# Output projection of a two-layer hybrid trunk: one chunk each of four groups first, with their last states gated before the final scans

## The chip, the core and the metric

One core of a Trainium2 chip runs the whole program: TensorE (PE, with its weight loads listed as PEld), VectorE (DVE), ScalarE (ACT), GpSimd (POOL) and SyncE (SP), which issues the DMAs of the stretch treated here. The metric is the device time of one execution in microseconds (us). The kernel before takes 2250.49 us (median of three runs, 2247.55 to 2251.17).

## The reference

Layer 0 is a gated linear attention, layer 1 an RG-LRU. Only the end of layer 1 matters here:

```
proj = h @ w_in                        # h: [2048 latent + 256 context, 1024]
z, g = split(proj, [1280])
z = conv4(z) + bias
r, i = sigmoid(z @ w_a + b_a), sigmoid(z @ w_x + b_x)     # 5 blocks of 256 channels
a = exp(-8 * r * softplus(-lam));  u = sqrt(1 - a*a) * (i * z)
h_t = a_t * h_{t-1} + u_t              # forwards (hf) and backwards (hb), column-major over the grid
y = ((hf + hb) * silu(g)) @ w_out      # [2048, 1280] @ [1280, 1024]
out = x + gate * rms_norm(y)
```

The latent grid has 32 rows and 64 columns; the scans run column by column, so position `32*c + r` of a scanned channel is row r of column c.

## The kernel before

All products are made in three matmuls of split operands (`mm_step`, L272 to L275: hi x hi, hi x lo, lo x hi). Channels lie on partitions: the 1280 channels are five blocks `b` of two tiles each, so w_out has ten slices k = 0 to 9 (`NLT`), two per block, and each slice has two halves `nh` of 512 output columns. The 2048 rows of the output are eight groups `g` of 256 (four grid rows each); a group has two chunks `i` of 128 rows: i = 0 takes grid columns 0 to 31, i = 1 columns 32 to 63.

**Block by block.** For each block, `proj_block` projects z and the gate branch g (one unit `u` of rows after another; the copies of the g part go through tiles tagged `gs`, L1057, and are stored to `g1d`, L1058), `mix` makes the two scans, and `gate` (blocks 0 to 3 only) multiplies silu(g) with the summed states and stores to `ogd`. `mix` of block b runs woven into `proj_block` of block b+1. `mix` has two directions d of two halves hb each: it makes the r and i gates piece by piece (PE, then sigmoids at L979), then for the whole half tanh, sqrt and exp on ACT (each kind behind a table load), two products on DVE (L1158, L1159), and the scans (L1166 forwards, L1170 backwards). The backward scan adds its result to `hf` (L1175). In the backward direction the half hb = 0 covers grid columns 32 to 63 and hb = 1 columns 0 to 31.

**Partial sums.** While `mix` of the last block (b = 4) runs, `part_gen` sums k = 0 to 3 (`KPART` = 4) for all 16 chunks and stores the partial results to `ypd`. Its activations come in pages: `og_page` (L1199 on) loads a page of two k-slices of 256 rows from `ogd` into a tile `gs` (named og, L1210), casts it on ACT (hi, L1212), subtracts on DVE (lo, L1214). The hi and lo tiles lie in the pool `wA` (32 buffers), next to the slices of w_out. The pool `p3` gives `gs` two buffers, and the pages, the copies of `proj_block` and whatever else carries the tag share these two. For the last block (b = 4) nothing is stored: `og_page` loads `g1d` (L1204), applies Silu (L1205), multiplies with the rows of `hf` (L1208) and then splits.

**The weave.** `weave(prev, part_gen(), 1.0)` takes one step of `mix`, then one of `part_gen`. `mix` has 18 steps; step 17 of `part_gen` is the first of group 4, in which it asks for the two pages of group 5 and for slices 7 and 8 of w_out. The last stretch of `mix` (the tables and scans of d = 1, hb = 1) is `mix`'s step 18. The rest of `part_gen`, with the pages of groups 6 and 7, is written out after it.

**Order.** The program's text gives the order of tile requests; the framework then fixes, before the run, the order of the instructions of each engine from a simulated timeline, so an engine may run instructions well ahead of or behind the text. A tile gets one of its tag's buffers when one is free.

**The end.** Eight PSUM banks (`banks`) are filled with k = 4 to 7 of chunks 0 to 3 (groups 0 and 1) before the last block's pages exist (`pre`). Then the loop over groups adds k = 8, 9 for these, makes k = 4 to 9 for the others, and finishes each chunk: add the partial sum (L1310), multiply by the gate row (L1311), sum of squares on ACT (L1314), the rstd (L165 to L177), add x (L1323), store.

Of the kernel before, what the change touches and what calls it, by code (L numbers as in the profile page):

```python
# [9 lines left out]
F32 = mybir.dt.float32  # L10
F32R = mybir.dt.float32r
I32 = mybir.dt.int32
AF = mybir.ActivationFunctionType
ALU = mybir.AluOpType
# [3 lines left out]
P = 128  # L18
# [45 lines left out]
def kernel(ctx, tc, x, c, cx, c_ctx, ada_w, ada_b, norm_pre, norm_post,  # L64
# [17 lines left out]
    def mk(p, tag, shape, dtype=F32, bufs=None, name=None):  # L82
        uid[0] += 1
        kw = {} if bufs is None else {"bufs": bufs}
        return p.tile(list(shape), dtype, tag=tag, name=f"{name or tag}_{uid[0]}", **kw)
# [186 lines left out]
    def mm_step(o_, a, b, first, last):  # L272
        PE.matmul(o_, a[0], b[0], start=first, stop=False)  # L273
        PE.matmul(o_, a[0], b[1], start=False, stop=False)  # L274
        PE.matmul(o_, a[1], b[0], start=False, stop=last)  # L275
# [682 lines left out]
    if True:  # L958
# [27 lines left out]
        def load_wo(p, k, tag="w"):  # L986
            return [load_split(p, lru_w_out[0, k * P:(k + 1) * P, nh * 512:(nh + 1) * 512], [512], tag, name="wo")
                    for nh in range(2)]
# [107 lines left out]
        def mix(b, zs, pend, res):  # L1096
# [3 lines left out]
            for d in range(2):  # L1100
# [5 lines left out]
                for hb, pieces in enumerate(halves):  # L1106
# [39 lines left out]
                    if d == 0 and hb == 0:  # L1146
                        yield from pend
                        hf = [mk(qh, "hf", [P, T]) for t in range(2)]
                    TT = [mk(q1, "TT", [P, 1280], bufs=2) for t in range(2)]
                    kts = [2 * b + t for t in range(2)]  # L1150
                    for t in range(2):
# [5 lines left out]
                    for t in range(2):  # L1157
                        V.scalar_tensor_tensor(TT[t][:, 0:n], R[t][:, 0:n], 1.0, TT[t][:, 0:n], op0=ALU.add, op1=ALU.mult)  # L1158
                        V.tensor_tensor(I[t][:, 0:n], I[t][:, 0:n], TT[t][:, 0:n], op=ALU.mult)  # L1159
                    for t in range(2):  # L1160
                        for (a, w), o_ in zip(pieces, offp):
                            init = 0.0 if tail[t] is None else tail[t]
                            ac, ic = R[t][:, o_:o_ + w], I[t][:, o_:o_ + w]
                            if d == 0:
                                dst = hf[t][:, a - TC:a - TC + w] if a >= TC else ic
                                V.tensor_tensor_scan(out=dst, data0=ac, data1=ic, initial=init, op0=ALU.mult, op1=ALU.add)  # L1166
                                last = dst[:, w - 1:w]
                            else:
                                rv = [[-1, w]]
                                V.tensor_tensor_scan(out=vw(ic, w - 1, rv), data0=vw(ac, w - 1, rv), data1=vw(ic, w - 1, rv),  # L1170
                                                     initial=init, op0=ALU.mult, op1=ALU.add)
                                last = ic[:, 0:1]
                                if a >= TC:
                                    fs = hf[t][:, a - TC:a - TC + w]
                                    V.tensor_tensor(fs, fs, ic, op=ALU.add)  # L1175
                            tc_ = mk(q1, "tail", [P, 1], bufs=4)
                            V.tensor_copy(tc_, last)
                            tail[t] = tc_
# [21 lines left out]
        def og_page(p, g, b, pp, tag, nb=None):  # L1200
# [13 lines left out]
            V.tensor_tensor(lo, og, hi[:].bitcast(F32), op=ALU.subtract)  # L1214
            return hi, lo

        og0, wo = [], []
        for d in range(2):
            load_gate_w(0, d)
# [12 lines left out]
    with ExitStack() as s4:  # L1232
        pa = pool(s4, "p4a", 4, side="right")
        wpr = pool(s4, "wp4r", 4, side="right")

        def part_gen():

            sp = og0[0:2]
            for g in range(T // GT):
                nxt = None  # L1240
                if g + 1 < T // GT:
                    nxt = [og_page(p, g + 1, b_, wA, "w") for b_ in range(KPART // 2)]
                else:
                    og0.extend(og_page(p, 0, b_, wA, "w") for b_ in range(KPART // 2, NB - 1))
                if g == 0:
                    for k in range(KPART, 7):
                        wo.append(load_wo(wA if k < 6 else wpr, k))
                if g == T // GT // 2:

                    for k in (7, 8):  # L1250
                        wo.append(load_wo(qg, k, tag="gw"))
                for i in range(2):
                    n = 2 * g + i
                    for nh in range(2):
                        tg, nb = ("sc", 1) if (2 * n + nh) % 4 == 3 else ("pj", 3)
                        py = mk(ps, tg, [P, 512], bufs=nb)
                        mm3(py, [tuple(pg[:, k % 2, i * P:(i + 1) * P] for pg in sp[k // 2]) for k in range(KPART)],
                            [wo[k][nh] for k in range(KPART)])
                        yt = mk(pa, "yp", [P, 512])
                        (S.copy if nh else V.tensor_copy)(yt, py)  # L1260
                        st(ypd[n][:, nh * 512:nh * 512 + 512], yt)
                        yield
                sp = nxt

        weave(prev, part_gen(), 1.0)
        s5.close()
        del stages[3:]


        banks = [("pj", 3)] * 3 + [("uo", 2)] * 2 + [("sc", 1), ("sb", 1), ("tr", 1)]  # L1270

        def share(py, sp, i, nh, ks):
            for k in ks:
                mm_step(py, tuple(pg[:, k % 2, i * P:(i + 1) * P] for pg in sp[(k - KPART) // 2]), wo[k][nh],
                        k == KPART, k == NLT - 1)

        def bank(j):
            tg, nb = banks[j % 8]
            return mk(ps, tg, [P, 512], bufs=nb)

        sps = [og0[2:], [og_page(p, 1, b_, wA, "w") for b_ in range(KPART // 2, NB - 1)]]
        wo.append(load_wo(wA, 9))
        pre = []
        for n in range(4):
            for nh in range(2):
                pre.append(bank(len(pre)))
                share(pre[-1], sps[n // 2], n % 2, nh, range(KPART, 8))
        p = pool(s4, "p4", 2)
        grow = mk(p, "grow0", [P, 2, 512], bufs=1)
        ld(grow.rearrange("p a b -> p (a b)"), g1r)  # L1290
        pages = lambda g: (sps[g] if g < 2 else []) + [og_page(p, g, b_, p, "oh", 14)
                                                       for b_ in range(NB - 1 if g < 2 else KPART // 2, NB)]
        nxt = pages(0)
        for g in range(T // GT):
            sp, nxt = nxt, pages(g + 1) if g + 1 < T // GT else None
            for i in range(2):
                n = 2 * g + i
                xt = mk(p, "xt", [P, D])
                rows_of = lambda ap: ap.rearrange("(r c) d -> c r d", r=4)[32 * i:32 * i + 32]
                ld(xt, rows_of(x1d[g]))  # L1300
                yt = mk(p, "yt", [P, 2, 512])
                yf = yt.rearrange("p a b -> p (a b)")
                s2_ = mk(p, "s2", [P, 1], bufs=4)
                yp = mk(p, "ypl", [P, 2, 512])
                ld(yp.rearrange("p a b -> p (a b)"), ypd[n])
                for nh in range(2):
                    j = 2 * n + nh
                    py = pre[j] if j < 8 else bank(j)
                    share(py, sp, i, nh, range(8 if j < 8 else KPART, NLT))
                    V.tensor_tensor(yp[:, nh], py, yp[:, nh], op=ALU.add)  # L1310
                    V.tensor_tensor(yt[:, nh], yp[:, nh], grow[:, nh], op=ALU.mult)  # L1311
                jk = mk(p, "jk", [P, D], mybir.dt.bfloat16)
                if n + 1 < T // P:
                    S.activation(jk, yp.rearrange("p a b -> p (a b)"), AF.Square, accum_out=s2_)  # L1314
                else:
                    sh = mk(p, "sh", [P, 2], bufs=1)
                    for nh in range(2):
                        S.activation(jk[:, nh * 512:nh * 512 + 512], yp[:, nh], AF.Square, accum_out=sh[:, nh:nh + 1])
                    V.tensor_tensor(s2_, sh[:, 0:1], sh[:, 1:2], op=ALU.add)
                rs = rstd_of(p, s2_, 1, 1.0 / D, "yn")  # L1320
                w = D if n + 1 < T // P else 512
                for o_ in range(0, D, w):
                    V.scalar_tensor_tensor(yf[:, o_:o_ + w], yf[:, o_:o_ + w], rs, xt[:, o_:o_ + w], op0=ALU.mult, op1=ALU.add)  # L1323
                    st(rows_of(out[0][g * GT:(g + 1) * GT])[:, :, o_:o_ + w], yf[:, o_:o_ + w])
# [31 lines left out]
```

## Time and profile before

| | us |
|---|---|
| median of three runs | 2250.49 |
| profiled execution, device time | 2249.55 |
| its span, first to last instruction | 2247.8 |
| PE busy in the span | 2159.2 (96%) |
| DVE busy | 1683.7 (75%) |
| ACT busy | 1333.8 (59%) |
| mean granted TensorE clock | 0.987 |

The share of busy time is an average over stages. The change touches only the last 300 us, so the profile is read there: first the busy time by stretches, then the order in time of the engines around each hole in PE's work. In a timeline a row gives the start, the duration, the engine, the line, the operation, the tiles (out<-in), and in brackets the idle time before it with what ended it. "issue" rows of SP are the time in which the DMA was put into its queue, not its transfer.

### The profile page before, as it was taken

To read this page: it belongs to the slowest core of one execution; us is meant where nothing else is said; L and a number is where in the kernel's file an instruction comes from. 1 tells how busy PE (TensorE), PEld (TensorE's weight loads), DVE (VectorE), ACT (ScalarE), POOL (GpSimd) and SP (SyncE) were. 2 spreads that over 40 slices of the span, in tenths; PEclk is the share of its full clock that TensorE was granted. 3 is DMA by queue.
4 is the path that set the end of the run, shared out by engine and by line. 5 is a ranking of instruction groups with operands and counts; after the bars stand their busy time and mean duration, and the time that the engine had idled before them with its cause. 6 is when DMAs were issued, how large, how long until landed. Compare 5 with 4: busy or idle time off the path is not lost.

```text
span 2247.8 us, 40378 instructions
## 1 busy us (share of the span) xinstructions
PE 2159.2 (96%) x14935; PEld 1769.1 (79%) x14935; DVE 1683.7 (75%) x4043; ACT 1333.8 (59%) x2508; POOL 83.5 (4%) x173
## 2 busy tenths in 40 slices
PE   6999999999999999989999999999999999999898
PEld 3888888888877887877777788878887878777686
DVE  3898988898876987958887235684686766967687
ACT  4767676665544554545776436756757757747531
POOL 1000000000000000000000000000000000000000
PEclk9999999999999999999999999999999999999999
DMA  9322233344245324367886862365354463442276
GB/s 311 125 94 99 91 110 126 114 129 130 87 169 171 126 99 154 125 226 244 280 284 217 297 238 98 136 216 197 104 190 148 131 213 125 159 164 99 90 259 227
DMA packets 212725, 370.93 MB, mean 165 GB/s; under 512 B 22818, under 2 KB 90624, under 8 KB 212528
## 3 DMA queue, kind: packets, MB, share of 16 engines
q1 hardware_dynamic: 202544, 336.61, 44.9%
q0 software_dynamic: 9120, 30.44, 3.6%
q8 instruction: 117, 1.92, 0.3%
q10 hardware_dynamic: 864, 1.31, 0.2%
q14 instruction: 80, 0.66, 0.1%
HBM read 250.54 MB, written 117.74 MB: 164 GB/s over the span
## 4 chain that ended last, share of the span: by engine, by line
PE 73%; DVE 9%; DMA 8%; ACT 7%; issue 2%; SPq 0%; DVEq 0%; ACTq 0%
PE pj L273 15%; PE pj L274 15%; PE pj L275 15%; PE uo L273 3%; PE uo L275 3%; PE uo L274 3%; DMA h<-h0d 2%; PE sc L538 2%; ACT TT L979 2%; DMA TT<-g1d 2%; ACT L979 1%; PE sc L273 1%; PE sc L274 1%; PE sc L275 1%; PE tr L261 1%
## 5 line engine op out<-in xcount | busy, mean ns | idle before, releaser
L274 PE MATMUL pj<-h,w 128*128 128x256 f32 (+1 forms) x1120 | 372.8, 333 | 7.8 <-DMA h<-h0d 5.5
L273 PE MATMUL pj<-h,w 128*128 128x256 f32 (+1 forms) x1120 | 373.1, 335 | 3.8 <-ACT zc L1054 2.2
L275 PE MATMUL pj<-h,w 128*128 128x256 f32 (+1 forms) x1120 | 370.1, 331 | 0.0
L274 PEld LDWEIGHTS pj<-h,w 128*128 128x128 f32 x1120 | 212.5, 190 | 33.1 <-DMA h<-h0d 7.7
L273 PEld LDWEIGHTS pj<-h,w 128*128 128x128 f32 x1120 | 212.6, 190 | 30.0 <-ACT zc L1054 2.5
L273 PE MATMUL pj<-w,h 128*128 128x512 f32 (+1 forms) x592 | 232.0, 394 | 0.0
L274 PE MATMUL pj<-w,h 128*128 128x512 f32 (+1 forms) x592 | 230.7, 390 | 0.0
L275 PE MATMUL pj<-w,h 128*128 128x512 f32 (+1 forms) x592 | 229.8, 388 | 0.0
L275 PEld LDWEIGHTS pj<-h,w 128*128 128x128 f32 x1120 | 212.3, 190 | 19.9
L273 PE MATMUL pj<-wo,oh 128*128 128x512 f32 x424 | 173.0, 409 | 16.8 <-ACT oh L1212 9.2
L551 ACT ACTIVATE E<-E 128x512 f32<-128x512 f32 x216 | 135.1, 632 | 75.0 <-DVE E L548 71.0
L274 PE MATMUL pj<-wo,oh 128*128 128x512 f32 x424 | 169.6, 400 | 0.0
L275 PE MATMUL pj<-wo,oh 128*128 128x512 f32 x424 | 168.6, 401 | 0.1
L552 DVE TENSOR_TENSOR E<-QK,E 128x512 f32<-128x512 f32 x216 | 142.4, 682 | 4.4 <-ACT E L551 4.0
L275 PEld LDWEIGHTS pj<-w,h 128*128 128x128 f32 x592 | 111.2, 188 | 21.6
L273 PEld LDWEIGHTS pj<-w,h 128*128 128x128 f32 x592 | 111.0, 188 | 21.6
L274 PEld LDWEIGHTS pj<-w,h 128*128 128x128 f32 x592 | 111.3, 188 | 20.8
L546 DVE TENSOR_TENSOR E<-xc 128x256 f32<-128x256 f32 (+1 forms) x252 | 100.6, 399 | 29.6 <-PE tr L584 17.1
L1158 DVE SCALAR_TENSOR_TENSOR TT<-R,TT 128x1280 f32<-128x1280 f32 (+1 forms) x40 | 52.5, 1355 | 91.7 <-ACT R L979 91.7
L273 PEld LDWEIGHTS pj<-wo,oh 128*128 128x128 f32 x424 | 80.7, 190 | 37.3 <-ACT oh L1212 9.7
L1142 DVE TENSOR_TENSOR I<-I,zc 128x512 f32<-128x512 f32 (+1 forms) x100 | 62.9, 632 | 57.8 <-ACT I L979 57.3
L979 ACT ACTIVATE TT<-TT 128x512 f32<-128x512 f32 (+2 forms) x72 | 65.3, 926 | 59.9 <-DMA TT<-g1d 59.2
(353 smaller groups left out, 5269.7 us busy)
## 6 DMA issues: line engine op xcount, KB each, us to landing
h<-h1d SPq DMA_DIRECT2D x296, 256.0 KB
defd<-de POOLq DMA_DIRECT2D x64, 320.0 KB, 2.6
de<-defd SPq DMA_DIRECT2D x64, 320.0 KB
h0d<-h SPq DMA_DIRECT2D x72, 256.0 KB
h<-h0d SPq DMA_DIRECT2D x72, 256.0 KB
h1d<-h SPq DMA_DIRECT2D x72, 256.0 KB
xt<-in_x_dram SPq DMA_DIRECT2D x32, 512.0 KB
xt<-in_ada_w_dram SPq DMA_DIRECT2D x32, 512.0 KB
```

Source lines behind the costliest of these rows:

```text
L261: PE.transpose(to, xh[i][kk * P // w][:, kk * P % w:kk * P % w + P], ident if mixed is None else mixed)
L273: PE.matmul(o_, a[0], b[0], start=first, stop=False)
L274: PE.matmul(o_, a[0], b[1], start=False, stop=False)
L275: PE.matmul(o_, a[1], b[0], start=False, stop=last)
L538: PE.matmul(dst, lk[:, i * P + w * a:i * P + w * a + w], lq[:, i * P + w * b:i * P + w * b + w], start=True, stop=True, tile_position=(0, ...
L546: V.tensor_tensor(vw(E, s, [[256, nq], [2 * s, nb], [1, s]]), vw(X, 1 + s, [[256, nq], [2 * s, nb], [1, s]]), vw(X, s, [[257, nq], [2 * s, ...
L551: S.activation(E, E, AF.Exp, scale=-1.0 / 16)
L552: V.tensor_tensor(E, QK, E, op=ALU.mult)
L979: ins = S.activation(*a, **kw).ins
L1142: V.tensor_tensor(I[t][:, o_:o_ + w], I[t][:, o_:o_ + w], zsl(t, a, w), op=ALU.mult)
L1158: V.scalar_tensor_tensor(TT[t][:, 0:n], R[t][:, 0:n], 1.0, TT[t][:, 0:n], op0=ALU.add, op1=ALU.mult)
```

## The change

- `og_half` is a page of the last block for one chunk: 128 rows of both k-slices instead of 256. It loads through a `gs` tile of whichever pool `p` names at that time, applies Silu, multiplies with the rows of `hf` of this chunk alone, and puts hi and lo into one tile.
- `early` makes the four halves i = 1 of groups 0 to 3. It is called in `mix` of the last block, in its last half (d = 1, hb = 1), ahead of the scans. Their hi and lo tiles take the four `gw` buffers that the backward gate weights leave. At that place `p` is the pool `p3`.
- Slice 8 of w_out moves from `gw` to `wA`, and is loaded with slice 9 after the pages.
- Ahead of the last loop, the pages k = 4 to 7 of groups 0 to 3 are made (before: groups 0 and 1), and the eight banks take chunk i = 1 of groups 0 to 3 instead of both chunks of groups 0 and 1: first k = 4 to 7 for all, then k = 8, 9 from the early halves.
- The last loop finishes these four chunks first, then chunk 0 of groups 0 to 3, then groups 4 to 7. The halves i = 0 are made in the first four turns.

```diff
@@ mix
                         hf = [mk(qh, "hf", [P, T]) for t in range(2)]
+                        hf_now[:] = [hf]
...
                         V.tensor_tensor(I[t][:, 0:n], I[t][:, 0:n], TT[t][:, 0:n], op=ALU.mult)
+                    if b == NB - 1 and d + hb == 2:
+                        early()
                     for t in range(2):
@@ new
+        def og_half(pp, tag, nb, g, i):
+            og = mk(p, "gs", [P, 2, GT], name="og")[:, :, 0:P]
+            ld(og, g1d[NB - 1][:, :, g * GT + i * P:g * GT + i * P + P])
+            S.activation(og, og, AF.Silu)
+            for t in range(2):
+                orow = og[:, t].rearrange("p (c r) -> p c r", r=4)
+                V.tensor_tensor(orow, orow, vw(res[0][t], 4 * g + 32 * i * ROWS, [[ROWS, 32], [1, 4]]), op=ALU.mult)
+            pg = mk(pp, tag, [P, 2, 2, P], F32R, bufs=nb, name="oh")
+            S.copy(pg[:, 0], og)
+            V.tensor_tensor(pg[:, 1], og, pg[:, 0].bitcast(F32), op=ALU.subtract)
+            return pg
+        def early():
+            res.append(hf_now[0])
+            for g in range(4):
+                halves[g, 1] = og_half(qg, "gw", 8, g, 1)
+            res.clear()
@@ part_gen
-                    for k in (7, 8):
-                        wo.append(load_wo(qg, k, tag="gw"))
+                    wo.append(load_wo(qg, 7, tag="gw"))
@@ after the weave
-        sps = [og0[2:], [og_page(p, 1, b_, wA, "w") for b_ in range(KPART // 2, NB - 1)]]
-        wo.append(load_wo(wA, 9))
-        for n in range(4):
+        full[0] = og0[2:]
+        for g in range(1, 4):
+            full[g] = [og_page(p, g, b_, wA, "w") for b_ in range(KPART // 2, NB - 1)]
+        for k in (8, 9):
+            wo.append(load_wo(wA, k))
+        for g in range(4):
             for nh in range(2):
                 pre.append(bank(len(pre)))
-                share(pre[-1], sps[n // 2], n % 2, nh, range(KPART, 8))
+                share(pre[-1], g, 1, nh, range(KPART, 8))
+        for g in range(4):
+            for nh in range(2):
+                share(pre[2 * g + nh], g, 1, nh, range(8, NLT))
...
+        order = [(g, 1) for g in range(4)] + [(g, 0) for g in range(4)] + [(g, i) for g in range(4, 8) for i in range(2)]
+        for n_, (g, i) in enumerate(order):
+            if 1 <= n_ < 5:
+                halves[n_ - 1, 0] = og_half(p, "oh", 14, n_ - 1, 0)
+            if n_ in (5, 7, 9, 11):
+                full[(n_ + 3) // 2] = [og_page(p, (n_ + 3) // 2, b_, p, "oh", 14) for b_ in range(KPART // 2, NB)]
```

## Rows read from the trace of the kernel before

**Rows 1.** Busy time by stretch, all engines; the first line names the columns.

```profile
core 0: us, PE busy (x) PEld busy (x) DVE busy (x) ACT busy (x) POOL busy (x), PEclk, DMA share, GB/s
2110.00:2120.00 10.00, 6.11 (x27) 4.59 (x25) 8.49 (x10) 4.94 (x6) 0.00 (x0) 0.94 0.10 35
2120.00:2130.00 10.00, 4.66 (x13) 3.70 (x14) 6.51 (x13) 1.24 (x2) 0.00 (x0) 0.55 0.46 162
```

**Rows 2.** Timeline of PE: around its last hole, and its last matmul.

```profile
2115.71 0.40 PE L275 MATMUL tr<-wo,oh 128*128 128x512 f32 x1
...
2125.34 0.79 PE L273 MATMUL pj<-wo,oh 128*128 128x512 f32 x1 [9.23 <-ACT oh L1212]
...
2129.24 0.39 PE L274 MATMUL uo<-wo,oh 128*128 128x512 f32 x1
...
2238.70 0.39 PE L275 MATMUL tr<-wo,oh 128*128 128x512 f32 x1
```

**Rows 3.** Chain of waits ahead of that matmul: start, us, what.

```profile
2100.85 0.69 DVE hf L1175
...
2113.87 2.27 DVE I L1159 x2
...
2123.92 0.68 DVE og L1208 x2
2124.67 0.63 ACT oh L1212
```

**Rows 4.** Timeline of ACT: uses of the two gs buffers, 1857 to 1946 us.

```profile
1857.83 0.60 ACT L1057 COPY gs<-sc 128x512 f32<-128x512 f32 x1
...
1913.71 1.08 ACT L1057 COPY gs<-pj 128x512 f32<-128x512 f32 x2
...
1922.73 0.61 ACT L1212 CAST oh<-og 128x512 fp32r<-128x512 f32 x1
...
1945.81 1.05 ACT L1057 COPY gs<-pj 128x512 f32<-128x512 f32 x2
```

**Rows 5.** Instructions on tile og: xcount, duration ns min/median/max; DMA to landing (tile gs).

```profile
L1212 ACT CAST oh<-og x40: 603/620/633, 1921.6 to 2206.4; 128x512 fp32r<-128x512 f32 x40
L1214 DVE TENSOR_TENSOR oh<-og,oh x40: 665/683/694, 1923.1 to 2210.4; 128x512 fp32r<-128x512 f32 x40
L1208 DVE TENSOR_TENSOR og<-og,hf x16: 414/418/426, 2123.8 to 2205.9; 128x256 f32<-128x256 f32 x16
DMA to landing us min/median/max: 2.0/2.8/6.7
```

**Rows 6.** Timeline of SP: stores from gs, loads of pages, loads of w_out.

```profile
1869.81 2.87 SPq L198 DMA_DIRECT2D stg<-in_lru_w_out_dram  x2
...
1914.33 0.81 SPq L1058 DMA_DIRECT2D g1d<-gs  x2
...
1918.04 1.29 SPq L1210 DMA_DIRECT2D og<-ogd  x2
...
1928.70 16.02 SPq L198 DMA_DIRECT2D stg<-in_lru_w_out_dram  x6
...
1949.31 1.28 SPq L1210 DMA_DIRECT2D og<-ogd  x2
...
2020.46 0.54 SPq L1210 DMA_DIRECT2D og<-ogd  x1
...
2028.73 0.53 SPq L1210 DMA_DIRECT2D og<-ogd  x1
```

**Rows 7.** Timeline of PE: last matmul of group 5's partial sums, first of group 6's.

```profile
2049.25 0.40 PE L275 MATMUL sc<-wo,oh 128*128 128x512 f32 x1
2049.49 0.39 PE L273 MATMUL pj<-wo,oh 128*128 128x512 f32 x1
```

**Rows 8.** Timeline of ACT: behind the last exp of the last half.

```profile
2112.53 1.28 ACT L1205 ACT_TABLE_LOAD   x1
2113.83 1.15 ACT L1205 ACTIVATE og<-og 128x512 f32<-128x512 f32 x2
```

More of the change, by code (lines that the diff above doesn't have):

```diff
@@ L1215, in og_page @@
             return hi, lo
+        def og_half(pp, tag, nb, g, i):
[9 more added lines that the diff above has]
+            return pg
+        halves = {}
+        def early():
[3 more added lines that the diff above has]
+            res.clear()
+        hf_now = []
         og0, wo = [], []
@@ L1270, with share @@
         banks = [("pj", 3)] * 3 + [("uo", 2)] * 2 + [("sc", 1), ("sb", 1), ("tr", 1)]
-        def share(py, sp, i, nh, ks):
+        full = {}
+        def share(py, g, i, nh, ks):
             for k in ks:
-                mm_step(py, tuple(pg[:, k % 2, i * P:(i + 1) * P] for pg in sp[(k - KPART) // 2]), wo[k][nh],
-                        k == KPART, k == NLT - 1)
+                if k >= KPART + 4 and (g, i) in halves:
+                    pg = halves[g, i]
+                    act_ = (pg[:, 0, k % 2], pg[:, 1, k % 2])
+                else:
+                    act_ = tuple(q[:, k % 2, i * P:(i + 1) * P] for q in full[g][(k - KPART) // 2])
+                mm_step(py, act_, wo[k][nh], k == KPART, k == NLT - 1)
         def bank(j):
@@ L1290 @@
         ld(grow.rearrange("p a b -> p (a b)"), g1r)
[L1291 to L1296, printed above, removed]
+        order = [(g, 1) for g in range(4)] + [(g, 0) for g in range(4)] + [(g, i) for g in range(4, 8) for i in range(2)]
[4 more added lines that the diff above has]
+                full[(n_ + 3) // 2] = [og_page(p, (n_ + 3) // 2, b_, p, "oh", 14) for b_ in range(KPART // 2, NB)]
+            if True:
                 n = 2 * g + i
@@ L1306 @@
                 for nh in range(2):
-                    j = 2 * n + nh
-                    py = pre[j] if j < 8 else bank(j)
-                    share(py, sp, i, nh, range(8 if j < 8 else KPART, NLT))
+                    j = 2 * n_ + nh
+                    if j < 8:
+                        py = pre[j]
+                    else:
+                        py = bank(j)
+                        share(py, g, i, nh, range(KPART, NLT))
                     V.tensor_tensor(yp[:, nh], py, yp[:, nh], op=ALU.add)
```

## The prediction

> **What bounds the kernel now.** I read the busy time by stretches first, then PE's timeline, then the chain of waits, then the timelines of SP and ACT. PE is full nearly everywhere in the last 200 us, except in one hole: 6.11 of 10 us busy in the one stretch and 4.66 in the next, where the granted clock falls to 0.55 [rows 1]. PE stops at 2116.1 us, when the eight banks hold all that needs no last state, and goes on at 2125.34, after 9.23 us of waiting for a cast of ScalarE [rows 2]. Ten matmuls then take 3.90 us up to 2129.24, the first of them at half clock; from there to 2239.1 there are 470 matmuls, 0.2337 us each, so the slow ones cost 3.90 - 2.34 = 1.6 us. The hole is worth 9.2 + 1.6 = 10.8 us at most. The chain in front of it is the second half of the last backward scan: product L1159, scans, multiplication with `hf` (L1208), cast (L1212) [rows 3]. But the states of columns 32 to 63 are final far earlier, with the last L1175 of the first half, at 2101.5 us. The change works on these.
>
> **Part 1, the aim.** No matmul is added or removed: 96 go into the banks for k = 4 to 7 as before, and 48 (4 groups x 2 halves x 2 slices x 3) become ready ahead of the last scans, 11.2 us at 0.2337. They would cover the hole of 9.2. This is the gain that can be had; whether it comes is decided by part 2.
>
> **Part 2, the two `gs` buffers.** Each early half first needs a `gs` tile of pool `p3`, which has two, and its text stands ahead of the pages of groups 6 and 7. What does the trace say of the order in which buffers are given? The copies of the g part left both buffers by about 1861 (1857.83 and 0.60, and a store of 2.8 us [rows 4, 5]), and the next copies came at 1913.71. In between both buffers were empty for 50 us, and the first two pages, whose data in `ogd` were long complete, were not loaded: their loads come at 1918.04, just behind the stores of the copies that precede them in the text. SP was not the reason; it issued loads of w_out, which stand later in the text, at 1869.81 [rows 6]. The same a second time: casts of these pages at 1922.73, next copies at 1945.81, next pages only at 1949.31, six loads of w_out in between [rows 4, 6]. So the buffers of one tag are given in the order of the text, even while they lie empty.
>
> In the text the early halves (step 18 of `mix`) stand behind step 17 of `part_gen`, which asks for group 5's pages, and ahead of all of its later steps. Before, two loads take the buffers at 2020.46 and 2028.73: group 6's pages, the thirteenth and fourteenth loads of the twenty before the hole [rows 6]. After, these places belong to early halves 0 and 1, whose inputs in `g1d` are complete. They then sit in both buffers until `hf` is final, near 2100, and halves 2 and 3 come next in the same buffers. Only behind them come group 6's pages. PE finishes group 5's partial sums at about 2049.5 and begins group 6's there [rows 7]; it would have only gate matmuls from then on.
>
> **When does PE go on?** The first half's states are final at 2101.5 [rows 3]. Without the pages of groups 7, 0 and 1, DVE loses six L1214 of 0.68 = 4.1 us before that; against this, Silu of two halves brought forward between sigmoids costs a table load there and one back, each 1.30 from its start to the next instruction [rows 8], at two moments, 5.2 us. That bounds it between 2097.4 and 2106.7; I take 2099, nearer the lower end since a Silu can also stand in a wait. Then:
> - Halves 0, 1: each two multiplications of half the size of L1208 (0.42; between 0.21 and 0.42, I take 0.3), a cast of half of 0.62 (0.4) and a subtraction of half of 0.68 (0.42) [rows 5]: 1.4 us for the first, 2100.4.
> - Halves 2, 3: transfer 2.8 [rows 5], 2103.2. Silu early at a table load of 1.30 and 0.4, then 1.4: 2106.3. Or Silu behind the exps as in the trace [rows 8]: DVE is then at L1159, which ends at 2116.1 - 2.5 = 2113.6, and 1.4 more gives 2115.1 [rows 3].
> - Group 6's first page: transfer 2.8, cast 0.62, subtraction 0.68 = 4.1: 2110.4 or 2119.2.
>
> The two ends lie equally near to rows; I take 2115.
>
> **The sum.** From group 6 on PE has 96 matmuls of partial sums, 96 for the banks and 480 for the rest, 672 x 0.2337 = 157.0 us, and 1.6 of slow clock after the halt. End of PE: 2115 + 158.6 = 2273.6. Before, its end is 2239.1 in a span of 2247.8; the same 8.7 us behind it give a span of 2282.3, and the 1.75 us between span and the profiled execution's time (2249.55) give 2284.1. The median of the runs, 2250.49, is 0.9 above that execution; I leave this in the range. **Forecast: 2284 us.**
>
> In this sum the hole of 9.2 us is already gone: by the time that the banks are full the last scans are long over. What is late next are the pages: a pair takes 4.1 to 5 us through two buffers, and PE needs a new pair each 24 matmuls, 5.6 us, so it should not stop again. The extra pages of groups 2 and 3 (4 casts, 4 subtractions) then lie beside PE's partial sums, at nothing if DVE keeps up, else 4 x 0.68 = 2.7 us. Slice 8 in `wA` instead of `gw` is loaded beside the same sums: nothing, or a wait of one transfer, 2.8. The halves instead of pages in the last loop are four more issues on SP (0.53 each [rows 6]) of half the bytes, behind PE's 432 remaining matmuls: nothing, or 2.1. The transfers of the last loop (rows of x, partial sums, results) are the same.
>
> A rule weighed: a table load for Silu shows 1.30 us to the next instruction [rows 8]. The Trainium skill, "ScalarE: Activation LUTs", section "What ACT_TABLE_LOAD costs", counts 2.66 us for each switch, a drain included. By that the late way would take 1.36 more, and the sum about 2285; this trace doesn't show the drain.
>
> **Rivals.**
> 1. *Buffers go to whom is ready* (other side: faster). Then group 6 keeps its pages and the early halves get buffers later. Silu stands behind the exps, L1159 ends at 2116.1, the first half is ready 1.4 later at 2117.6, and PE waits 1.5 instead of 9.2 and keeps its clock: 2249.55 - 7.7 - 1.6 = 2240. The later halves come in time (2.8 us of matmuls for each group). The four halves put 4 x 1.02 = 4.1 us ahead of the scans, which end at 2128, when the 48 matmuls end also, at 2128.8. For it: the aim of part 1 is sound. Against: both empty stretches of part 2. It decides at whether a page load (L1210 before) for group 6 is issued by about 2035. 2238 to 2246.
> 2. *No difference*: as in 1, but Silu is drawn into the sigmoids at two moments, 5.2 us, and the 4.1 ahead of the scans falls on the end of the chain: 9.3 against 9.3, 2250.
> 3. *Slower still*: after the halt, DVE takes the scans and L1159 ahead of the pages' subtractions. The scans of the last half fill 2116.1 to 2123.9; a page behind them lets PE start at 2125 or later, and one more wait of the pages of up to 8 us follows: 2294 to 2304.
>
> **Chances.** The forecast with its own range, 2275 to 2295 (start of PE at 2106 to 2126): 0.65. Rival 1: 0.15. Rival 2: 0.05. Rival 3: 0.15. A measurement of this kernel can tell about 0.2%, 4.5 us, from no change. So faster 0.15, same 0.05, slower 0.80. The range 2266 to 2304 holds the forecast's case and rival 3, with some room below for a start of PE as early as 2098; the faster cases are left out.
>
> **What would show it.** Right: in the timeline of SP two loads og<-g1d of the early halves near 2020 and 2029, none of og<-ogd between there and 2100; PE with gate matmuls only from about 2050 to 2115, at a low clock; then no hole until the end. Step by step: last L1175 of the first half near 2099; group 6's first partial sum near 2115; last matmul near 2274. Wrong: group 6's sums at 2050 as before, and early casts near 2117. Then rival 1 holds, and what failed is the reading that buffers follow the text.

## The result and the profile after

| | before | after |
|---|---|---|
| median of 4 runs, us | 2250.83 | 2288.92 |
| lowest to highest, us | 2247.55 to 2256.91 | 2285.48 to 2296.77 |
| profiled execution, device time | 2249.55 | 2292.11 |
| its span | 2247.8 | 2290.3 |
| PE busy | 2159.2 (96%) | 2172.6 (95%) |
| mean granted TensorE clock | 0.987 | 0.976 |

The changed kernel is slower: 1.0174 times the time of before, with a 95% interval of 1.0155 to 1.0194. The forecast was 2284.

Two profiled executions can't be laid over each other by their start, since executions of one kernel differ by more than 10 us and some of that arises in program text that is the same. I use a mark instead: the last stores of the g part (the issue g1d<-gs behind the copies of 1945.81 [rows 4]). It is at 1946.41 us before and at 1955.03 after. "Aligned" below means: after's time less 8.62. From the mark to the end of the span are 301.4 us before and 335.3 after, 33.9 more; the medians differ by 38.1. A figure "from the mark on" always comes from the one execution that was profiled, and its own spread is not known.

SP after, the loads of tile og alone. L1213 is the load of a page, L1223 that of a half; compare [rows 6], where two pages were loaded at 2020.46 and 2028.73:

```profile
2005.62 0.53 SPq L1213 DMA_DIRECT2D og<-ogd  x1
2013.01 0.53 SPq L1213 DMA_DIRECT2D og<-ogd  x1
...
2027.54 0.54 SPq L1223 DMA_DIRECT2D og<-g1d  x1
...
2037.52 0.53 SPq L1223 DMA_DIRECT2D og<-g1d  x1
...
2103.85 1.30 SPq L1223 DMA_DIRECT2D og<-g1d  x2
...
2120.35 10.10 SPq L1213 DMA_DIRECT2D og<-ogd  x5
```

No page is loaded between 2013 and 2120. PE's timeline after, some matmuls with waits ahead of them, and its last; L1215 is the cast of a page:

```profile
2088.68 0.79 PE L273 MATMUL uo<-zh,gw 128*128 128x512 f32 x1 [6.74 <-ACT R L979]
...
2102.82 0.79 PE L273 MATMUL sb<-zh,gw 128*128 128x512 f32 x1 [3.35 <-ACT I L979]
2124.19 0.80 PE L273 MATMUL pj<-wo,oh 128*128 128x512 f32 x1 [18.44 <-ACT oh L1215]
...
2281.49 0.40 PE L275 MATMUL tr<-wo,oh 128*128 128x512 f32 x1
```

The wait of 9.23 us for a page of the last block, at 2125.34 [rows 2], is gone. In its place there is one of 18.44 us for the first page of group 6's partial sums, and ahead of it PE waits for gate inputs (uo, tr and sb, 23.6 us in all from 2020 on, where before has one such wait, of 4.3 us). The stretches of after; for the columns see [rows 1]:

```profile
2080.00:2090.00 10.00, 3.26 (x12) 2.41 (x11) 5.28 (x5) 8.58 (x8) 0.00 (x0) 0.83 0.00 0
2090.00:2100.00 10.00, 7.47 (x16) 4.34 (x15) 9.86 (x19) 4.29 (x6) 0.00 (x0) 0.50 0.00 0
2100.00:2110.00 10.00, 2.93 (x6) 1.82 (x6) 4.33 (x11) 6.00 (x9) 0.00 (x0) 0.50 0.09 27
2110.00:2120.00 10.00, 0.00 (x0) 0.00 (x0) 4.61 (x7) 9.04 (x10) 0.00 (x0) 0.50 0.00 0
2120.00:2130.00 10.00, 5.81 (x19) 4.70 (x20) 9.30 (x16) 2.26 (x4) 0.00 (x0) 0.62 0.32 99
```

PE thins out, its granted clock falls to the lower level (0.50), and the DMA share is 0.00 in three stretches: nothing is being fetched that PE could work on. From 2130 to 2280 every stretch has PE busy 10.00.

From the mark to the last matmul's end PE makes the same 1170 matmuls in both kernels; before, then after:

```profile
1946.41:2239.09 292.68, 275.11 (x1170) 221.57 (x1169) 224.00 (x446) 145.34 (x215) 0.00 (x0) 0.97 0.51 174
1955.03:2281.89 326.86, 282.22 (x1170) 224.57 (x1169) 230.72 (x458) 152.79 (x227) 0.00 (x0) 0.92 0.46 156
```

So of the 34.2 us between the two stretches 27.1 are idle time of PE (44.6 against 17.6), and 7.1 are the same matmuls at a lower mean clock (0.92 against 0.97).

### The profile page after: what moved, and what is told of

Its sections match the earlier page's. It is cut to its first block, busy times and chain, and to the rows that moved or that the text cites. A ratio compares the mean times of both kernels' runs of the same rounds, so it can differ in the third digit from the quotient of the medians.

```text
span 2290.3 us, 40403 instructions
## 1 busy us (share of the span) xinstructions
PE 2172.6 (95%) x14935; PEld 1778.5 (78%) x14935; DVE 1690.6 (74%) x4055; ACT 1342.7 (59%) x2520; POOL 83.7 (4%) x173
## 4 chain that ended last, share of the span: by engine, by line
PE 71%; DVE 10%; DMA 8%; ACT 8%; issue 2%; SPq 0%; DVEq 0%; ACTq 0%
PE pj L273 15%; PE pj L274 15%; PE pj L275 14%; PE uo L273 3%; PE uo L275 3%; PE uo L274 3%; PE sc L538 2%; DMA h<-h0d 2%; DMA ogd<-TT 2%; ACT TT L979 2%; ACT L979 1%; PE sc L274 1%; PE sc L275 1%; DMA TT<-g1d 1%; PE sc L273 1%
## 5 line engine op out<-in xcount | busy, mean ns | idle before, releaser
L273 PEld LDWEIGHTS pj<-wo,oh 128*128 128x128 f32 x424 | 80.9, 191 | 42.9 <-ACT oh L1215 19.2
L273 PE MATMUL uo<-zh,gw 128*128 128x512 f32 (+1 forms) x200 | 77.9, 391 | 28.9 <-ACT R L979 28.8
```

## Experiments

Theory A: the early halves hold both `gs` buffers until `hf` is final, and the pages behind them in the text starve. Theory B: the time is lost by the other edits (order of the last loop, choice of banks, Silu between sigmoids). The last column is the span from the mark on, less the 301.4 us of before. The expectations were written against the 2250.49 us of the kernel before; in the two later series it stands at 2254.15 and 2254.73.

| run | median, us | lowest to highest, runs | before in the same series | ratio (95% interval) | from the mark on, us |
|---|---|---|---|---|---|
| after | 2288.92 | 2285.48 to 2296.77, 4 | 2250.83 | 1.0174 (1.0155 to 1.0194) | +33.9 |
| hold2 | 2275.01 | 2269.94 to 2279.81, 4 | 2254.15 | 1.0082 (1.005 to 1.0114) | +23.0 |
| two2 | 2280.97 | 2278.44 to 2288.83, 4 | 2254.15 | 1.0105 (1.0075 to 1.0134) | +25.3 |
| textlate | 2261.0 | 2257.3 to 2266.68, 10 | 2254.15 | 1.0024 (1.001 to 1.0038) | +5.6 |
| own4 | 2249.22 | 2243.84 to 2255.23, 10 | 2254.15 | 0.9977 (0.996 to 0.9994) | -6.6 |
| one1 | 2273.74 | 2272.09 to 2275.61, 4 | 2254.73 | 1.0083 (1.0061 to 1.0106) | +18.2 |
| own2 | 2258.92 | 2248.23 to 2265.34, 10 | 2254.73 | 1.0012 (0.9996 to 1.0028) | +1.0 |
| evac3 | 2247.12 | 2238.59 to 2254.95, 12 | 2254.73 | 0.9963 (0.9944 to 0.9981) | -9.5 |
| evac3pin | 2248.83 | 2239.97 to 2252.83, 12 | 2254.73 | 0.9967 (0.9953 to 0.9982) | -12.3 |

### hold2: the holding alone, in the kernel before

```diff
                     if b == NB - 1 and d + hb == 2:
+                        for g in range(2):
+                            og = mk(p, "gs", [P, 2, GT], name="og")[:, :, 0:P]
+                            ld(og, g1d[NB - 1][:, :, g * GT + P:g * GT + 2 * P])
+                            for t in range(2):
+                                orow = og[:, t].rearrange("p (c r) -> p c r", r=4)
+                                V.tensor_tensor(orow, orow, vw(hf[t], 4 * g + 32 * ROWS, [[ROWS, 32], [1, 4]]), op=ALU.mult)
```

The two tiles are used for nothing; everything else is the kernel before.

> The kernel before with one addition: at the place of the early halves two tiles gs are loaded from g1d and multiplied with the final states, and not used further (no Silu, no cast, no change of the last loop). The output is that of the kernel before. Theory A: the holding alone makes the halt; PE goes on near 2100, time 2265 to 2275. Theory B (order of the last loop, table loads): 2250 to 2253, the price of four small products.

SP of this kernel, tile og alone (L1163 the holders, L1217 the pages):

```profile
2028.53 0.54 SPq L1163 DMA_DIRECT2D og<-g1d  x1
...
2036.78 0.53 SPq L1163 DMA_DIRECT2D og<-g1d  x1
...
2106.51 16.28 SPq L1217 DMA_DIRECT2D og<-ogd  x5
```

PE of hold2 behind the halt:

```profile
2110.55 0.80 PE L273 MATMUL pj<-wo,oh 128*128 128x512 f32 x1 [0.62 <-ACT oh L1219]
```

The halt of after appears in the kernel before as soon as two tiles that wait for `hf` are asked for at this place: no page for 70 us behind the second holder, waits of PE for gate inputs as in after (the longest 6.7 us in both), and 23.0 us more from the mark on. The long wait of 18.44 us does not appear: the pages are loaded as soon as the holders are done, and PE goes on at 2110.55. Of the 23.1 us more up to the last matmul only 9.7 are idle time of PE; the rest is the same 1170 matmuls in 288.54 us instead of 275.11, at a mean granted clock of 0.91. No early sum, no bank, no Silu and no new last loop is in this kernel, so theory B can't explain these 23 us; the other 10.9 of after hold2 leaves open. The time lies at the upper end of my range for theory A, 2265 to 2275.

### two2 and one1: fewer early halves

The early calls cover two groups (two2) or one (one1); the others are written out behind the weave, but ahead of the pages k = 4 to 7 of groups 0 to 3:

```diff
-            for g in range(4):
+            for g in range(2):        # one1: range(1)
                 halves[g, 1] = og_half(qg, "gw", 8, g, 1)
...
+        for g in range(2, 4):         # one1: range(1, 4)
+            halves[g, 1] = og_half(qg, "gw", 8, g, 1)
```

> The changed kernel with only two early halves ahead of the last scans (groups 0 and 1); those of groups 2 and 3 are written after the weave. Theory A: both buffers are still held until the last states of columns 32 to 63 are final, but there is no second pair of loads behind them: PE goes on about 16 us earlier than in the changed kernel (2104 + 2.8 transfer + cast against 2124), time 2268 to 2277. Theory B, price by the work ahead of the scans: two halves of 1 us each less, 2286 to 2288.

> Only group 0's half is made early; those of groups 1 to 3 are written out behind the pages. It holds one of the two gs buffers until hf is final (near 2100), the other stays free. Theory A (the halt comes from gs buffers held by tiles that wait for hf, and a free buffer goes to the next request of the text): group 6's pages pass one by one through the other buffer, 2.8 + 0.62 + 0.68 = 4.1 us each, 8.2 a pair against 5.6 us of matmuls, so PE lags some 2.6 us a group instead of halting; pages are loaded between 2020 and 2100; 2250 to 2265 us. Theory A' (buffers are given strictly in rotation): one page passes, the next waits for the held buffer, no load of a page until near 2100, as with two holders: 2270 to 2285. Theory B (the order of the last loop or of the banks costs the time): 2280 or more, as with all four.

SP of two2, tile og:

```profile
2032.11 0.54 SPq L1223 DMA_DIRECT2D og<-g1d  x1
...
2042.09 0.53 SPq L1223 DMA_DIRECT2D og<-g1d  x1
...
2110.33 19.62 SPq L1213 DMA_DIRECT2D og<-ogd  x6
```

PE, then ACT of two2 at the end of the halt:

```profile
2120.31 0.79 PE L273 MATMUL pj<-wo,oh 128*128 128x512 f32 x1 [8.09 <-ACT oh L1215]
```

```profile
2119.66 1.12 ACT L1215 CAST oh<-og 128x512 fp32r<-128x512 f32 x2
```

Two are enough for the halt; all four cost 8.6 us more from the mark on (33.9 - 25.3), and the intervals of the two ratios lie apart. From hold2 to two2, which has all other edits of the change, the step is 2.3 us, by one execution of each. My range of 2268 to 2277 was missed. The pages are loaded right behind the last states, at 2110.33, as I had expected, but their cast stands in ACT's order behind the square roots and exps of the last half and starts only at 2119.66. So PE goes on 9.3 us earlier than in after (159.85 us behind the mark instead of 169.16), and not 16. SP of one1, tile og:

```profile
2024.00 0.54 SPq L1223 DMA_DIRECT2D og<-g1d  x1
...
2033.97 0.53 SPq L1213 DMA_DIRECT2D og<-ogd  x1
...
2039.08 0.53 SPq L1213 DMA_DIRECT2D og<-ogd  x1
...
2075.21 0.53 SPq L1223 DMA_DIRECT2D og<-g1d  x1
...
2112.06 1.22 SPq L1223 DMA_DIRECT2D og<-g1d  x2
...
2127.97 6.01 SPq L1213 DMA_DIRECT2D og<-ogd  x3
```

PE of one1 at the end of its halt:

```profile
2131.74 0.79 PE L273 MATMUL pj<-wo,oh 128*128 128x512 f32 x1 [19.22 <-ACT oh L1215]
```

I had expected 2250 to 2265 by theory A, and 2270 to 2285 if buffers were given strictly in rotation. The time lies in the second range, but the trace refutes rotation: with one buffer held from 2024 on, pages pass through the other, 5.1 us apart (2033.97, 2039.08). What I had overlooked is the place in the text of the other halves: group 1's takes the free buffer at 2075.21, both are held again, and the same halt follows, with 19.2 us for PE at its end. So a free buffer goes to the next request of the text, whoever that is; one1 by itself doesn't tell what a single held buffer would cost.

### textlate: the early halves behind all pages in the text

```diff
-                    if b == NB - 1 and d + hb == 2:
-                        early()
...
             full[g] = [og_page(p, g, b_, wA, "w") for b_ in range(KPART // 2, NB - 1)]
+        early()
         for k in (8, 9):
```

> The changed kernel with one edit: the four early halves are written out after all pages k = 4 to 7, instead of ahead of the last scans; the same loads, casts, products and the same order of the last loop. Theory A (the two gs buffers are given in the order of the text, so that the early halves keep them from the pages of groups 6 and 7): no halt of PE between 2050 and 2120, group 6's pages are loaded near 2020 to 2040 as before, time 2238 to 2250. Theory B (the halt is the price of the other parts: the new order of the last loop, the early Silu and products): 2280 or more.

SP of textlate, tile og (L1210 the pages, L1220 the halves), then its PE:

```profile
2023.42 0.54 SPq L1210 DMA_DIRECT2D og<-ogd  x1
2031.68 0.53 SPq L1210 DMA_DIRECT2D og<-ogd  x1
...
2103.18 2.89 SPq L1220 DMA_DIRECT2D og<-g1d  x2
2116.01 1.18 SPq L1220 DMA_DIRECT2D og<-g1d  x2
```

```profile
2114.37 0.80 PE L273 MATMUL sb<-zh,gw 128*128 128x512 f32 x1 [4.77 <-ACT I L979]
2145.74 0.80 PE L273 MATMUL pj<-wo,oh 128*128 128x512 f32 x1 [6.61 <-DVE ypl L1347]
```

Moving one call in the text takes 28.3 of the 33.9 us away, so the halt is the order of the requests. The pages are loaded as before (2023.42 and 2031.68 are 2019.3 and 2027.6 aligned, 4.11 taken off). But the time lies above my range of 2238 to 2250, and the kernel doesn't win: through two buffers the halves are loaded in two pairs, at 2103 and 2116, and two smaller holes are left, 4.77 and 6.61 us. Here a part of theory B can be seen at work: ACT runs the Silu of the halves between the last half's sigmoids, in three turns, each with a table load of 1.28 us to Silu and one back (Silu at 2106.99, 2111.90 and 2119.93). The last scans are 13.9 us later from the mark on than before (the last addition to `hf` ends at 191.35 us behind it, before at 177.45); what share of this the table loads make was not tried.

### own4 and own2: buffers of their own

```diff
-            og = mk(p, "gs", [P, 2, GT], name="og")[:, :, 0:P]
+            if i:
+                og = mk(pe, "ge", [P, 2, P], name="og")
+            else:
+                og = mk(p, "gs", [P, 2, GT], name="og")[:, :, 0:P]
...
-        pa = pool(s4, "p4a", 4, side="right")
+        pa = pool(s4, "p4a", 3, side="right")      # own4 alone
...
+        pe = pool(s4, "p4e", 4, side="right")      # own2: 2
```

`p4a` gives up one of its buffers to make room for the four.

> The changed kernel with the early halves in four buffers of their own (the pool of the partial results gives up one of four for it), written at the same place ahead of the last scans. Theory A: no halt, 2238 to 2250; the four loads then come as soon as the buffers are there, so Silu may come early as well and cost table loads of 1.3 us. Theory B (work ahead of the scans, order of the loop): 2280 or more.

> The early halves take two buffers of a pool of their own, gs is left to the pages. Theory A: group 6's pages are loaded at 2020 and 2029 as before, no halt from 2050 to 2115; halves 0 and 1 get Silu early, halves 2 and 3 only when 0 and 1 are done, near 2105 to 2118, so the banks' last matmuls of groups 2 and 3 may come up to 5 us late: 2247 to 2254 us. Theory B: 2275 or more.

With four buffers the pages come about where they were, at 2019.89 and 2028.15 (2018.2 and 2026.4 aligned, 1.74 taken off), the four Silu share one table load at 1956.14, and PE runs without a wait for pages. The kernel is 0.23% faster than before (0.06% to 0.4%). One hole is left; own4's PE, and DVE around it:

```profile
2131.46 0.79 PE L273 MATMUL pj<-wo,oh 128*128 128x512 f32 x1 [4.34 <-DVE ypl L1356]
```

```profile
2126.83 0.69 DVE L1178 TENSOR_TENSOR hf<-hf,I 128x512 f32<-128x512 f32 x1
...
2130.72 1.29 DVE L1356 TENSOR_TENSOR ypl<-pj,ypl 128x512 f32<-128x512 f32 x2 [3.13 <-DMA ypl<-ypd]
```

All eight banks are summed up and none is empty. The first is emptied by the addition at 2130.72, which waits for its partial sum `ypl`; that transfer is issued at 2126.87, 0.08 us behind the end of the last scan. In the text the pool of `ypl` is opened only when the pools of `mix` are closed; that it lies in memory which the last scans still use is read from this and from the same 0.07 to 0.08 us in textlate and own2, and was not tried by itself. So a part of the gain of "summed up whole in eight banks" is given back at the next step: the banks are full before anybody may empty them.

With two buffers the halves 2 and 3 come in the second turn, and their Silu stands ahead of the last half's tables. ACT of own2:

```profile
2120.48 1.28 ACT L1227 ACT_TABLE_LOAD   x1 [3.05 <-DMA og<-g1d]
2121.78 0.72 ACT L1227 ACTIVATE og<-og 128x256 f32<-128x256 f32 x2
...
2123.55 1.28 ACT L979 ACT_TABLE_LOAD   x1
```

The last addition to `hf` ends 8.3 us later than in own4 (2134.06 and 2125.78 aligned, by 9.95 and 1.74), and the wait for `ypl` is 8.46 us instead of 4.34. My range of 2247 to 2254 left this out; the kernel is no different from before within its interval.

### evac3 and evac3pin: banks emptied without ypl

evac3 is own4 with three banks copied by ACT:

```diff
+                    if j < 3:
+                        ev = mk(pa, "yp", [P, 512])
+                        S.copy(ev, py)
+                        py = ev
```

evac3pin also gives the halves of chunk 0 buffers of `pe`, with their Silu tied behind the last exps:

```diff
-            og = mk(p, "gs", [P, 2, GT], name="og")[:, :, 0:P]
+            og = mk(pe, "ge", [P, 2, P], name="og")
...
-            S.activation(og, og, AF.Silu)
+            if i:
+                S.activation(og, og, AF.Silu)
+            else:
+                act("silu", og, og, AF.Silu)
```

> Early halves in four buffers of their own, and the first three banks of the last loop are copied by ScalarE into tiles of SBUF before DVE adds the partial sum, so that a bank comes free without the load of ypl, whose memory is free only when the last scans have ended. Theory A (the 4.3 us hole left at 2131 us is the wait for a bank, and so for ypl): the hole goes, with its slow clock of about 1 us: 2244 to 2246 us, 0.2% below the same kernel without the copies. Rival: the halves of chunk 0, whose states are final only with the last scans, are late at the same place; the hole stays with another name, 2248 to 2250.

> As the kernel with three banks copied, and the halves of chunk 0 also load through the four buffers of their own, so that their data wait in SBUF when the last states are final, with their Silu held behind the last exps. Theory A: if after the copies the chunk 0 halves end last, 1 to 3 us less than with the copies alone, 2241 to 2245 us. Rival: PE is full there already, no difference, 2244 to 2246.

ACT of evac3 ahead of the last scans' end, and its stretches at the place of the hole:

```profile
2119.16 0.59 ACT L1358 COPY yp<-pj 128x512 f32<-128x512 f32 x1 [1.17 <-PE pj L275]
...
2121.98 0.59 ACT L1358 COPY yp<-pj 128x512 f32<-128x512 f32 x1 [0.82 <-PE pj L275]
```

```profile
2120.00:2130.00 10.00, 10.00 (x45) 8.04 (x44) 9.32 (x15) 1.18 (x2) 0.00 (x0) 1.00 0.03 5
2130.00:2140.00 10.00, 10.00 (x45) 8.06 (x44) 6.48 (x17) 5.03 (x10) 0.00 (x0) 1.00 0.75 245
```

Three banks are free at 2122.6, the hole is gone and the clock stays at 1.00: that the hole was the wait for a bank is shown. From the mark on the kernel takes 2.9 us less than own4 and 9.5 less than before; against before it is 0.37% faster (0.19% to 0.56%). What the copies are worth in time is less sure, since the intervals of evac3 and own4 overlap. Its median is 1 us above the range that I gave, in a series in which before stands at 2254.73 and not at 2250. The rival, that chunk 0's halves are late at the same place, falls: the hole did not come back under another name, and having their data in SBUF (evac3pin) changes nothing that the two intervals tell apart. So evac3pin's rival (no difference) holds, though its median of 2248.83 lies above both ranges that I gave.

## Why the prediction was right

- **The `gs` buffers.** Right, as written: two halves at 2027.54 and 2037.52 (2018.9 and 2028.9 aligned, where the pages of group 6 were [rows 6]), none of ogd up to 2120.35, and no partial sum between the end of group 5's, near 2058, and 2124.19. Only the clock was not low all that time: it is 1.00 from 2040 to 2080 and falls to 0.50 behind that. hold2 shows it without the rest of the change, textlate and own4 take it away in two ways, and one1 shows that it is the order of the requests, not a rotation.
- **When PE goes on.** 2124.19, aligned 2115.6; the forecast was 2115. That it comes so near is luck. The value was a middle of two ways (2110.4 and 2119.2), neither of which happened, and two errors cancel:

DVE, then ACT of after around the halves:

```profile
2101.29 0.69 DVE L1178 TENSOR_TENSOR hf<-hf,I 128x512 f32<-128x512 f32 x1
2102.01 0.49 DVE L1227 TENSOR_TENSOR og<-og,hf 128x128 f32<-128x128 f32 x2
...
2103.41 0.75 DVE L1230 TENSOR_TENSOR oh<-og,oh 128x256 fp32r<-128x256 f32 x2
...
2119.91 0.41 DVE L1230 TENSOR_TENSOR oh<-og,oh 128x256 fp32r<-128x256 f32 x1
```

```profile
2107.88 0.42 ACT L1224 ACTIVATE og<-og 128x256 f32<-128x256 f32 x1
...
2114.91 2.19 ACT L979 ACTIVATE R<-R,lruc 128x1024 f32<-128x1024 f32 x2
2117.11 1.28 ACT L1224 ACT_TABLE_LOAD   x1
2118.41 0.42 ACT L1224 ACTIVATE og<-og 128x256 f32<-128x256 f32 x1
2118.73 0.39 ACT L1229 CAST oh<-og 128x256 fp32r<-128x256 f32 x1
...
2123.52 0.62 ACT L1215 CAST oh<-og 128x512 fp32r<-128x512 f32 x1 [3.04 <-DMA og<-ogd]
```

First, the states are final at 2101.98, aligned 2093.4: 8.2 us earlier than before, 5.6 earlier than the 2099 that I took, and below my lower bound of 2097.4. I had credited only six subtractions of DVE (4.1 us). The trace has eight fewer of them between the mark and the last states (10 instead of 18, since group 6's two are missing as well), and also four fewer copies of partial sums and two fewer subtractions for w_out; DVE is busy 109.28 us there instead of 117.25. PE is busy 10.72 of the 20 us from 2080 to 2100, where before it was full, so the gate matmuls wait for nothing but their input. How much either makes is open, since hold2 is as light on DVE (109.72) and has the same matmuls, and yet has its states only 2.2 us earlier than before (152.88 us behind the mark against 155.13). Its matmuls are slower: the granted clock from 2060 to 2080 is 0.55 and 0.77, in after 1.00.

Second, half 2 gets its Silu early (2107.88), as in the early way, but its cast stands behind sqrt, exp and four table loads until 2118.73. Its buffer is free at 2120.32, when its subtraction ends, 18.3 us behind the states; I had 7.3 in the early way and 16.1 in the late one. This mixed way I had not listed. The first page takes this buffer at once (2120.35) and needs 3.84 us from issue to PE (4.1 taken): PE starts on the hi part at 2124.19, before the subtraction at 2124.73. So 5.6 us too late for the states and 6.6 us too early for the buffer, measured from the middle of the two ways, nearly cancel.
- **The sum.** From 2124.19 to the last matmul's end at 2281.9 are 157.7 us (forecast 158.6; the slow clock cost 0.7 and not 1.6). The 1.6 was read a little low as well: nine matmuls and not ten start between 2125.34 and 2129.24 before, which makes 1.8. Behind it come 8.4 in the span and 1.8 outside (8.7 and 1.75). No further hole, as forecast. 2115.6 + 157.7 + 8.4 + 1.8 = 2283.5 on before's clock; the 8.6 us up to 2292.1 arose ahead of the mark.
- **Part 1 by itself.** The aim was put at 9.2 + 1.6 = 10.8 us at most. own4, evac3 and evac3pin get 6.6, 9.5 and 12.3 from the mark on, 4.9, 7.6 and 5.9 by medians; the 12.3 of one execution lie above this bound, the medians do not. Rival 1's 2240, some 10 us less than before, is what the idea comes near to when the pages keep their buffers and three banks are copied; it left out that a full bank must also be emptied.
- **The rule on table loads.** The last exp ends at 2117.10 and Silu begins at 2118.41, 1.3 us later. The 2.66 us of the Trainium skill ("ScalarE: Activation LUTs", section "What ACT_TABLE_LOAD costs") don't show in this switch; the measurement decides.

## What to carry to other kernels

A tile that is asked for early and waits long for its other input takes a buffer out of a shared pool for all of that time; price it by who is next in the text for the same tag, and what the main engine does without them. Give such tiles buffers of their own (or their request a later place) before you judge the idea behind them. And when sums are made ahead into all banks, look at what the first emptying of a bank waits for.

## What had not been expected

Executions reach the mark at very different times though the text ahead of it is the same: 1946.41 us (before), 1948.13 (evac3), 1955.03 (after), 1960.46 (two2). A part shows as granted clock: from 600 to 800 us PE was busy 197.68 of 200 at 1.00 before, and 195.30 at 0.98 after. What sets it was not tried; it is why differences below 1% are read here from the mark on and from the ratios of several runs.
